# 2 MB expert-weight blocks in 11 slots, zero-padded attention keys, another order of the last w2 products and of the final norm

## Chip, cores and metric

One NeuronCore of one Trainium2 chip runs the whole block. The metric is the device time of one execution in microseconds (us), the median of several runs.

## What is computed

The reference is one encoder layer on 512 tokens of width 1024, in float32. What matters here:

```python
xn   = rms_norm(h, norm_mix_w)
proj = xn @ w_in                      # 1024 x 9728: q/k/v of 24 attention heads, retention q/k/v/gate, branch gates
# branch A: 3 groups of 8 heads (head size 64); group 0 a window of +-64 tokens in token order,
#           groups 1 and 2 over tokens of equal residue mod 4 (and 16, by a mask)
scores = q @ k.T / 8 ; p = exp(scores - max) ; out = p @ v      # denominators combine the three groups
# branch B: retention, then both branches are gated, merged and projected by w_out
h   = h + merged @ w_out
hn  = rms_norm(h, norm_moe_w)
# mixture of experts: 64 experts, two per token out of one group of 8
hid = silu(xb @ w1[e]) * (xb @ w3[e]) ; y = hid @ w2[e]         # w1, w3: 1024 x 512, w2: 512 x 1024 each
out = rms_norm(h + sum(gate * y), norm_final_w)
```

Every expert gets tokens, so the 64 x 3 weight matrices of 2 MB each (384 MB in blocks of 1024 x 1024 bytes) are read once.

## The kernel before, in words

**Mixer.** Every projection goes through `project` (lines 242 to 281): weights come in chunks of 256 x 512 (`raw`, 512 KB, two buffers, DMA issued by SyncE at line 103), ScalarE and VectorE split each into a rounded part and a remainder (lines 212, 213), and TensorE multiplies three times (lines 267 to 269 for token-major results, 273 to 275 for transposed ones). The normalised input lies transposed in four tiles `xH0`, `xH1`, `xL0`, `xL1`; the same four hold the retention result and then the merged branches.

**Attention.** Per head group g the program projects q and k transposed, applies rotary (`rotary_to`: line 314 on VectorE, 315 and 316 on GpSimd), projects v, and then works through the query tiles. One score product has a contraction of 64: for g = 1, 2 (line 639) one product of 128 columns per head, 64 in all, with the odd head of a pair in partitions 64 to 127; for g = 0 (line 595) products of 192 columns. `probs` (lines 551, 553) adds the mask, takes the maximum and the exponential, `transposed_probs` (line 557) transposes, line 648 multiplies by v. These steps are mixed by the framework's scheduler with the products of the next projection, so that TensorE's queue is a fixed list in which a score product stands between projection products.

**Experts.** `experts(g)` handles four experts (32 token places each) at a time, 16 times. The tokens are gathered by one-hot products (line 769) into `xT`; then come 16 blocks of w1 and w3 (line 973) and 8 blocks of w2 (line 1026), each block 1 MB: 128 partitions, each one run of 8 KB. `wtile` gives each block a slot: 11 of pool `wA`, 2 halves of `big` (used once, later the result tile), `xH0`, `xL0`, `xH1`, `xL1` and `wB`; 18 for the first pass, 16 afterwards. A slot is loaded again as soon as the products that read it are done. All loads are issued by SyncE in program order (line 936), and a load waits for the eighth load before it. The w2 blocks hold 128 output columns each (`columns`); after them the result is split in two parts (lines 1009, 1010) and spread back to the tokens (`scatter`, lines 1017 to 1019). The last four experts do this in five column pieces of 256, 256, 256, 128 and 128, each product followed at once by its spread, with `finish` (line 1061) squaring for the norm.

**End.** `final` sums the squares, takes the root on GpSimd (line 152), multiplies by the norm weight (lines 1097 to 1100) and stores in seven pieces (lines 1102 and 1112).

The pools of the first loads lie where the attention's tiles lay, so the first weight load (program order: after five loads of w_out) waits until the mixer's last readers are done.

Of the kernel before, what the change touches and what calls it, by code (L numbers as in the profile page):

```python
# [10 lines left out]
F32 = mybir.dt.float32  # L11
# [26 lines left out]
NWA = 11  # L38
NK2 = 4
# [29 lines left out]
def hybrid_block(ctx, tc, a, out):  # L69
# [86 lines left out]
    class Halves:  # L156


        def __init__(self):
            self.t = []  # L160
            for i in range(2):
                t_ = xp.tile([P, 4, S], F32R, name=self.tag + "01"[i])
                self.t.append(t_)
# [7 lines left out]
    class Hi(Halves):  # L171
        tag = "xH"

    class Lo(Halves):
        tag = "xL"
# [11 lines left out]
    xH = Hi()  # L187
    xL = Lo()
# [106 lines left out]
    def rotary_to(dst, dilated):  # L295
# [4 lines left out]
        def evac(b, ps):  # L300
# [8 lines left out]
            for k in range(2):  # L309
# [6 lines left out]
                nc.gpsimd.tensor_tensor(d, d, w, op=ALU.add)  # L316
# [228 lines left out]
    rec0 = at.tile([P, NT, REC], F32, name="rec0")  # L545
    orders = (nat, dil4, dil4)
# [15 lines left out]
    def windows(qT, kT, v4):  # L562
# [14 lines left out]
        for t in range(NT):  # L577
# [9 lines left out]
            for slot, hh in enumerate((0, 1, 4, 5)):  # L587
                po = (hh % 2) * HD
                ps = tmp()
                sm = rp.tile([P, 512], F32, name="sd", bufs=6)  # L590
                for i in range(2):
                    cs = slice(i * W, (i + 1) * W)
                    blk = hh // 2 + i
                    for qs, k0 in parts_:
                        nc.tensor.matmul(ps[qs, cs], qT[po:po + HD, blk, t * P + qs.start:t * P + qs.stop],
                                         kT[po:po + HD, blk, k0:k0 + W], start=True, stop=True)
                    probs(rec, hh + 2 * i, ps[:, cs], sm[:, cs], masks[:, mo_:mo_ + W])
                prT = transposed_probs(ps, sm, 3)
                oc = slice(slot * (HD + 1), (slot + 1) * (HD + 1))
                for i in range(2):  # L600
                    full = slice(2 * i * P, (2 * i + 1) * P)
                    po = i * HD
                    for qs, k0 in parts_:
                        nc.tensor.matmul(po_ps[i][qs, oc], prT[:, full][:, qs],
                                         values(k0 + po, 0, P, hh + 2 * i), start=True, stop=False)
                    for qs, k0 in parts_:
                        nc.tensor.matmul(po_ps[i][qs, oc], prT[po:po + HD, P:2 * P][:, qs],
                                         values(k0 + (1 - i) * P, po, HD, hh + 2 * i), start=False, stop=True)
            for i in range(2):
                nc.scalar.copy(rec[:, :NH * (HD + 1)].rearrange("p (x z w) -> p x z w", x=2, z=2)[:, :, i],  # L610
                               po_ps[i][:, :4 * (HD + 1)].rearrange("p (x w) -> p x w", x=2))

    for g in range(3):
        qT, kT = qk_tiles()
        project_in(512 * g, None, rotary_to(qT, g > 0))
        project_in(1536 + 512 * g, None, rotary_to(kT, g > 0))
# [8 lines left out]
        if g == 0:  # L625
            windows(qT, kT, v4)
# [538 lines left out]
```

## Time and profile before

| | |
|---|---|
| median of 3 runs | 1665.96 us (1661.69 to 1669.53) |
| the profiled execution | 1663.84 us, its span 1662.1 us |
| TensorE busy | 1386.6 us (83%), 11699 instructions |
| VectorE, ScalarE, GpSimd busy | 561.7, 328.7, 182.4 us |
| granted TensorE clock, mean | 0.913 |
| moved by DMA | 476.56 MB in 98509 packets |

The page cuts the span into 40 slices of 41.55 us. Read it first for which engine is full where, then look at the stretches one by one: a busy share over the whole span says little, because the mixer and the experts have different limits. In the timelines a float32 product shows as two instructions, a rounded one (fp32r) as one. SPq is SyncE's queue, its rows are the moments at which DMAs are issued.

### The profile page before, as it was taken

Reading aid. Unit: us, or ns where it says so; the run is one execution under the profiler, and the core shown is the slowest. Engines: PE = TensorE matmul, PEld = TensorE weight load, DVE = VectorE, ACT = ScalarE, POOL = GpSimd, SP = SyncE. Lnnn points to the kernel's source line nnn. Section 1 sums busy time; section 2 is a strip of 40 time slices with the busy share of each in tenths; the row PEclk is TensorE's granted clock in tenths of the full one; section 3 lists DMA queues with packets and bytes.
Section 4 is the critical chain, followed back from the end, with each engine's and each line's share of the span. In section 5 each row is a group of like instructions: output and inputs, shape, how many; then the busy total and the mean of one; then the engine's idle time right before and its main releaser. Section 6 shows DMA issues by size and latency. Waiting matters only on the chain. (4 is left out here: it accounts for less than half of the span.)

```text
span 1662.1 us, 27242 instructions
## 1 busy us (share of the span) xinstructions
PE 1386.6 (83%) x11699; PEld 915.9 (55%) x11699; DVE 561.7 (34%) x1241; ACT 328.7 (20%) x618; POOL 182.4 (11%) x137
## 2 busy tenths in 40 slices
PE   7999999999999999988776776776776786687674
PEld 6878787686876778754442442342353354244243
DVE  7556463554634544442220120120221121022014
ACT  5332334334346333210000000000000000000002
POOL 2214260231502211000000000000000000000001
PEclk9999999999999999998987887897898788888787
DMA  6324343233323423989999999999999999999995
GB/s 179 111 77 105 91 137 90 77 102 96 96 90 90 141 76 107 398 341 421 421 421 422 422 422 422 422 421 422 422 421 421 422 422 422 421 422 421 422 421 213
DMA packets 98509, 476.56 MB, mean 287 GB/s; under 512 B 17296, under 2 KB 17808, under 8 KB 49168
## 3 DMA queue, kind: packets, MB, share of 16 engines
q1 hardware_dynamic: 97344, 474.76, 72.8%
q8 instruction: 94, 1.54, 0.4%
q14 instruction: 31, 0.25, 0.0%
q10 hardware_dynamic: 1040, 0.00, 0.0%
HBM read 459.96 MB, written 4.26 MB: 279 GB/s over the span
## 5 line engine op out<-in xcount | busy, mean ns | idle before, releaser
L973 PE MATMUL acc<-wa,xT 128*32 128x512 f32 x1408 | 212.4, 716 | 83.7 <-DMA wa<-in_moe_w_dram 83.7
L213 DVE SCALAR_TENSOR_TENSOR wL<-raw,nwx,wH 128x512 fp32r<-128x512 f32 x152 | 138.0, 937 | 106.8 <-ACT wH L212 106.6
L268 PE MATMUL acc<-xL,wH 128*128 128x512 f32 x416 | 172.0, 413 | 0.0
L267 PE MATMUL acc<-xH,wH 128*128 128x512 f32 x416 | 168.8, 406 | 1.2 <-ACT kT L667 1.2
L973 PEld LDWEIGHTS acc<-wa,xT 128*32 128x32 f32 x1408 | 37.7, 117 | 237.2 <-DMA wa<-in_moe_w_dram 176.2
L269 PE MATMUL acc<-xH,wL 128*128 128x512 f32 x416 | 168.0, 404 | 0.0
L1026 PE MATMUL acc<-wa,k 128*32 128x128 f32 x2816 | 113.9, 319 | 56.8 <-DMA wa<-in_moe_w2c_dram 52.4
L1026 PEld LDWEIGHTS acc<-wa,k 128*32 128x32 f32 x2816 | 89.0, 129 | 81.2 <-DMA wa<-in_moe_w2c_dram 65.0
L212 ACT ACTIVATE wH<-raw,nwx 128x512 fp32r<-128x512 f32 x152 | 103.1, 716 | 150.1 <-PE acc L275 55.8
L273 PE MATMUL acc<-wH,xH 128*128 128x512 f32 x320 | 127.6, 400 | 0.2 <-ACT rt L536 0.2
L274 PE MATMUL acc<-wL,xH 128*128 128x512 f32 x320 | 127.5, 398 | 0.1
L275 PE MATMUL acc<-wH,xL 128*128 128x512 f32 x320 | 127.4, 398 | 0.0
L994 DVE SCALAR_TENSOR_TENSOR k<-k,gsl,acc 128x512 f32<-128x512 f32 x16 | 12.0, 748 | 332.8 <-issue 283.2
L769 PE MATMUL tmp<-oh,h 128*128 128x128 f32 x960 | 110.6, 276 | 0.3 <-DVE big L1019 0.3
L769 PEld LDWEIGHTS tmp<-oh,h 128*128 128x128 f32 x960 | 108.7, 192 | 3.7 <-DVE big L1019 3.2
L152 POOL TENSOR_TENSOR rr<-rv,mhalf 128x1 f32<-128x1 f32 x8 | 4.9, 622 | 947.0 <-ACT jk L1061 935.9
L1010 DVE TENSOR_TENSOR xT<-acc,xT 128x512 fp32r<-128x512 f32 (+2 forms) x35 | 22.6, 646 | 231.9 <-ACT xT L1009 231.8
L267 PEld LDWEIGHTS acc<-xH,wH 128*128 128x128 f32 x416 | 78.4, 189 | 22.4 <-issue 2.5
L268 PEld LDWEIGHTS acc<-xL,wH 128*128 128x128 f32 x416 | 78.5, 189 | 21.5 <-issue 2.3
L269 PEld LDWEIGHTS acc<-xH,wL 128*128 128x128 f32 x416 | 78.5, 189 | 18.1 <-issue 1.5
L1019 DVE TENSOR_TENSOR big<-big,tmp 128x512 f32<-128x512 f32 (+2 forms) x132 | 76.6, 635 | 21.7 <-PE tmp L1018 21.7
L1017 PE MATMUL tmp<-xT,k 128*128 128x512 f32 (+2 forms) x140 | 61.5, 462 | 22.9 <-ACT xT L1009 22.1
(259 smaller groups left out, 1705.3 us busy)
## 6 DMA issues: line engine op xcount, KB each, us to landing
wa<-in_moe_w_dram SPq DMA_DIRECT2D x176, 1024.0 KB, 19.8
wa<-in_moe_w2c_dram SPq DMA_DIRECT2D x88, 1024.0 KB, 19.9
raw<-in_w_in_dram SPq DMA_DIRECT2D x76, 512.0 KB, 3.7
xH<-in_moe_w_dram SPq DMA_DIRECT2D x32, 1024.0 KB, 19.8
xL<-in_moe_w_dram SPq DMA_DIRECT2D x31, 1024.0 KB, 19.7
xL<-in_moe_w2c_dram SPq DMA_DIRECT2D x16, 1024.0 KB, 19.8
xH<-in_moe_w2c_dram SPq DMA_DIRECT2D x16, 1024.0 KB, 19.8
wB<-in_moe_w_dram SPq DMA_DIRECT2D x15, 1024.0 KB, 19.6
```

Source lines behind the costliest of these rows:

```text
L212: nc.scalar.activation(wH[:, k, :], raw[:, k, :], AF.Copy, scale=sc)
L213: nc.vector.scalar_tensor_tensor(wL[:, k, :], raw[:, k, :], sc, wH[:, k, :], op0=ALU.mult, op1=ALU.subtract)
L267: nc.tensor.matmul(ps[tt], wh[:, cs], srcH.blk(kt), **fl)
L268: nc.tensor.matmul(ps[tt], wh[:, cs], srcL.blk(kt), start=False, stop=False)
L269: nc.tensor.matmul(ps[tt], wl[:, cs], srcH.blk(kt), start=False, stop=(kt == nk - 1))
L273: nc.tensor.matmul(ps[tt], aH, wh, **fl)
L274: nc.tensor.matmul(ps[tt], aH, wl, start=False, stop=False)
L275: nc.tensor.matmul(ps[tt], aL, wh, start=False, stop=(kt == nk - 1))
L769: nc.tensor.matmul(gp[j // 4][:, (j % 4) * P:(j % 4 + 1) * P], h[:, t, j * P:(j + 1) * P], oh_t.rearrange("p e c -> p (e c)"), start=(t == ...
L973: nc.tensor.matmul(p_[e * CAP:(e + 1) * CAP, :], xT[:, j, e * CAP:(e + 1) * CAP], wt[:, e * FF:(e + 1) * FF], start=(j == 0), stop=(j == N ...
L1019: nc.vector.tensor_tensor(hs_[:, t, cs], (h if first else hs_)[:, t, cs], ps, op=ALU.add)
L1026: nc.tensor.matmul(py[e * CAP:(e + 1) * CAP, o:o + P], hdT[:, i, e * CAP:(e + 1) * CAP], w4[:, e, i, :], start=(i == 0), stop=(i == 3))
```

## The change

1. **Blocks.** w1 and w3 of one 128-row stretch come in one block: 2 MB, each partition one run of 16 KB (8 per four experts). w2 comes in 4 blocks by rows of the contraction (`moe_w2r`), so that each product has 512 columns and the result is complete only after the fourth block; for the last four experts the w2 blocks still hold columns (`moe_w2c`, 256 each, the last one loaded in two halves).
2. **Slots.** 11 slots of 2 MB: 5 of `wA`, `big` and `wk` once, `x0`, `x1` (each now holds the rounded and the remainder half of four blocks), 2 of `wB`; 9 from the second pass on. `xT`, the split result, the transposed one-hots and the hidden values have one buffer each; the last four lie in the place of `wk` after the first experts.
3. **Padded keys.** Rotary writes the keys to `kP`, 128 partitions by block, parity and token, zero in the other head's half. One product with a contraction of 128 gives the scores of both heads (256 columns for g = 1, 2; 384 for g = 0). GpSimd writes the two halves separately and clears the zeros once.
4. **Last experts.** A column piece's product is issued ahead of the spread before it.
5. **End.** GpSimd multiplies by the norm weight in `finish`, for all but the last 128 columns; in the last piece the squares of two of the four token tiles go to VectorE; one root for all four tiles; four stores of 512 KB.

```diff
-NWA = 11
-NK2 = 4
+NWA = 5
+NWB = 2
+SLOT = 4096
...
-                nc.gpsimd.tensor_tensor(d, d, w, op=ALU.add)
+                if pad is None:
+                    nc.gpsimd.tensor_tensor(d, d, w, op=ALU.add)
+                else:
+                    for z in range(2):
+                        hp = slice(z * HD, (z + 1) * HD)
+                        nc.gpsimd.tensor_tensor(pad[hp, b - 1 + k, z, :], d[hp], w[hp], op=ALU.add)
...
+    kP = at.tile([P, 4, 2, S], F32, name="kP")
+    for z in range(2):
+        nc.gpsimd.memset(kP[(1 - z) * HD:(2 - z) * HD, :, z, :], 0.0)
...
+                ts = slice(t * P, (t + 1) * P)
+                for i in range(0, 4, 2):
+                    nc.tensor.matmul(ps[:, i * P:(i + 2) * P], qT[:, (h0 + i) // 2, ts], kP[:, (h0 + i) // 2, :, ts],
+                                     start=True, stop=True)
                 for i in range(4):
-                    hh = h0 + i
-                    po = (hh % 2) * HD
                     cs = slice(i * P, (i + 1) * P)
-                    ts = slice(t * P, (t + 1) * P)
-                    nc.tensor.matmul(ps[:, cs], qT[po:po + HD, hh // 2, ts], kT[po:po + HD, hh // 2, ts],
-                                     start=True, stop=True)
-                    probs(rec, hh, ps[:, cs], sm[:, cs], masks[:, 3 * HD:3 * HD + P] if g == 1 else masks[:, 9 * HD:])
+                    probs(rec, h0 + i, ps[:, cs], sm[:, cs],
+                          masks[:, 3 * HD:3 * HD + P] if g == 1 else masks[:, 9 * HD:])
...
-    spare = [(xp, "xH0"), (xp, "xL0"), (xp, "xH1"), (xp, "xL1"), (mo, "wB")]
+    ring = [(wA, "wa")] * NWA + [(xp, "x0"), (xp, "x1")] + [(mo, "wB")] * NWB
+    once = [(big, "big"), (wk, "wk")]
+    slots = ring[:NWA] + once + ring[NWA:]
...
         for j in range(NK):
+            wt = load(block(w13, g, j)).rearrange("p (w e f) -> p w e f", w=2, e=EG)
             for w_, p_ in enumerate((p1, p3)):
-                wt = load(block(w13, g, 2 * j + w_))
                 for e in range(EG):
...
         if cols is None:
+            py = [acc(), acc()]
+            for i in range(4):
+                wt = load(block(w2r, g, i)).rearrange("p (e d) -> p e d", e=EG)
+                for hf in range(2):
+                    for e in range(EG):
+                        nc.tensor.matmul(py[hf][e * CAP:(e + 1) * CAP, :], hdT[:, i, e * CAP:(e + 1) * CAP],
+                                         wt[:, e, hf * 512:(hf + 1) * 512], start=(i == 0), stop=(i == 3))
...
-            for c0, n in cols:
-                py = acc()
-                for o in range(0, n, P):
-                    columns(wts[(c0 + o) // P], py, o)
-                cs = slice(c0, c0 + n)
-                split(cs, py[:, :n], nc.vector if n < 256 else nc.scalar)
-                scatter([cs])
-                finish(c0, n)
+            waits = []
+            for c in cols:
+                if c == cols[-1]:
+                    while waits:
+                        spread(*waits.pop(0))
+                waits.append((*c, product(*c)))
+                if len(waits) > 1:
+                    spread(*waits.pop(0))
+            spread(*waits.pop(0))
...
+            if i < len(last) - 1:
+                nc.gpsimd.tensor_tensor(o[t][:, cs], x, wf[:, cs], op=ALU.mult)
...
+        def rows(tt, eng):
+            rt = r[:, tt:tt + 1]
+            ts = slice(tt * P, (tt + 1) * P)
+            nc.vector.scalar_tensor_tensor(o[tt][:, c0:], res[0][:, tt, c0:], rt, wf[:, c0:], op0=ALU.mult,
+                                           op1=ALU.mult)
+            if eng is nc.scalar:
+                nc.scalar.activation(o[tt][:, :c0], o[tt][:, :c0], AF.Copy, scale=rt)
             else:
...
+                eng.tensor_scalar(o[tt][:, :c0], o[tt][:, :c0], rt, None, op0=ALU.mult)
+            nc.sync.dma_start(out=out[0, ts, :], in_=o[tt])
```

How TensorE's list changes in head group 1, from one `v` product (line 648) to the transposes. `sd` are the probabilities, `acc` rows are projection products. Before:

```order
L648 MATMUL tmp<-v,sd 64x65 x8
L639 MATMUL tmp<-kT,qT 128x128
L268 MATMUL acc<-xL_111,wH 128x512
L269 MATMUL acc<-xH_109,wL 128x512
L267 MATMUL acc<-xH_109,wH 128x512
L639 MATMUL tmp<-kT,qT 128x128
L268 MATMUL acc<-xL_111,wH 128x512
L269 MATMUL acc<-xH_109,wL 128x512
L267 MATMUL acc<-xH_109,wH 128x512
L639 MATMUL tmp<-kT,qT 128x128
```

and with the change:

```order
L657 MATMUL tmp<-v,sd 64x65 x8
L645 MATMUL tmp<-kP,qT 128x256 x2
L268 MATMUL acc<-x_109,wH 128x512
L269 MATMUL acc<-x_109,wL 128x512
L267 MATMUL acc<-x_109,wH 128x512
L268 MATMUL acc<-x_109,wH 128x512
L269 MATMUL acc<-x_109,wL 128x512
L267 MATMUL acc<-x_109,wH 128x512
L567 MATMUL tmp<-ident,sd 128x128 x3
```

Four score products, three of them alone between projection products, have become two that follow the `v` products directly.

SyncE's queue from the mixer's last loads to the second use of a slot. `raw` are mixer weights, `wk`, `wa`, `big`, `x_`, `wB` slots. Before:

```order
L103 DMA raw<-in_w_out_dram 128x2x512 x5
L936 DMA wa<-in_moe_w_dram 128x2048 x2
L103 DMA raw<-in_w_out_dram 128x2x512
...
L936 DMA wa<-in_moe_w_dram 128x2048 x7
L936 DMA big<-in_moe_w_dram 128x2048 x2
L936 DMA xH_5711<-in_moe_w_dram 128x2048
L936 DMA xL_5717<-in_moe_w_dram 128x2048
L936 DMA xH_5723<-in_moe_w_dram 128x2048
L936 DMA xL_5773<-in_moe_w2c_dram 128x2048
L936 DMA wB<-in_moe_w2c_dram 128x2048
L936 DMA wa<-in_moe_w2c_dram 128x2048 x6
```

and with the change:

```order
L942 DMA wk<-in_moe_w_dram 128x4096
L105 DMA raw<-in_w_in_dram 128x2x512 x3
...
L105 DMA raw<-in_w_out_dram 128x2x512 x5
L942 DMA wa<-in_moe_w_dram 128x4096
...
L942 DMA wa<-in_moe_w_dram 128x4096 x3
L942 DMA big<-in_moe_w_dram 128x4096
L942 DMA x_5657<-in_moe_w_dram 128x4096
L942 DMA x_5713<-in_moe_w2r_dram 128x4096
L942 DMA wB<-in_moe_w2r_dram 128x4096 x2
L942 DMA wa<-in_moe_w2r_dram 128x4096
```

One block (`wk`) is now loaded ahead of the mixer's last 23 weight chunks; the other first-pass blocks keep their place, and each row moves twice the bytes.

## Rows read from the trace of the kernel before

**Rows 1.** The page's 40 slices: busy tenths of TensorE and of the DMA engines.

```profile
PE   7999999999999999988776776776776786687674
DMA  6324343233323423989999999999999999999995
```

**Rows 2.** Stretches around the start of the expert weights: from:to, length, busy us of PE, PEld, DVE, ACT, POOL with their instruction counts, granted TensorE clock, mean DMA share, GB/s.

```profile
661.50:705.70 44.20, 44.05 (x280) 34.34 (x279) 16.97 (x50) 14.11 (x26) 1.12 (x2) 1.00 0.96 390
705.70:710.50 4.80, 4.42 (x41) 3.52 (x40) 4.16 (x25) 1.29 (x4) 0.55 (x1) 1.00 0.21 51
...
718.00:721.50 3.50, 3.50 (x35) 1.75 (x37) 3.09 (x20) 1.38 (x10) 0.00 (x0) 1.00 0.22 54
721.50:1635.00 913.50, 673.30 (x7845) 359.34 (x7837) 157.72 (x340) 47.92 (x93) 0.00 (x0) 0.85 1.01 420
```

**Rows 3.** SyncE's queue around the same place: start, length of the issue (or of several), what is loaded.

```profile
661.50 0.82 SPq L936 DMA_DIRECT2D wa<-in_moe_w_dram  x2
674.40 4.82 SPq L936 DMA_DIRECT2D wa<-in_moe_w_dram  x7
...
692.99 0.33 SPq L936 DMA_DIRECT2D xH<-in_moe_w_dram  x1
...
709.20 0.33 SPq L936 DMA_DIRECT2D xH<-in_moe_w_dram  x1
...
720.19 4.62 SPq L936 DMA_DIRECT2D wa<-in_moe_w2c_dram  x6
```

**Rows 4.** DMA packets of three stretches, in this order: 800 to 1600 us (8 KB runs only, full), 664 to 674 us (8 KB runs and the 2 KB runs of w_out, full), and 640 to 660 us (2 KB runs alone, not full; its second line gives the share of the engines' time).

```profile
DMA packets 46309, 337.20 MB, mean 422 GB/s; under 512 B 5137, under 2 KB 5137, under 8 KB 5265
...
DMA packets 966, 4.11 MB, mean 411 GB/s; under 512 B 80, under 2 KB 80, under 8 KB 592
...
DMA packets 823, 1.60 MB, mean 80 GB/s; under 512 B 48, under 2 KB 48, under 8 KB 822
q1 hardware_dynamic: 822, 1.59, 23.8%
```

**Rows 5.** TensorE in head group 1: start, length (from the first start to the modelled end), line, tile shape, result.

```profile
378.55 0.69 PE L648 MATMUL tmp<-v,sd 128*64 128x65 f32 x16
379.16 0.49 PE L639 MATMUL tmp<-kT,qT 64*128 64x128 f32 x2
379.58 0.50 PE L268 MATMUL acc<-xL,wH 128*128 128x512 f32 x1
379.92 0.40 PE L269 MATMUL acc<-xH,wL 128*128 128x512 f32 x1
380.15 0.39 PE L267 MATMUL acc<-xH,wH 128*128 128x512 f32 x1
380.47 0.49 PE L639 MATMUL tmp<-kT,qT 64*128 64x128 f32 x2
380.89 0.50 PE L268 MATMUL acc<-xL,wH 128*128 128x512 f32 x1
```

**Rows 6.** Groups by line and shape: count, busy us, mean ns, idle time before.

```profile
L639 PE MATMUL tmp<-kT,qT 64*128 64x128 f32 x128 | 31.1, 323 | 0.2 <-DVE rec L551 0.2
L447 POOL MEMSET yret<- 64x1024 f32 x1 | 1.1, 1132 | 0.0
```

**Rows 7.** A run of full-array float32 products of 128 columns (the gather), and what starts after it.

```profile
1588.99 7.41 PE L769 MATMUL tmp<-oh,h 128*128 128x128 f32 x64
1596.33 4.50 PE L973 MATMUL acc<-wa,xT 128*32 128x512 f32 x40
```

**Rows 8.** Who TensorE waited for between 200 and 660 us, the longest in total: us, times, longest.

```profile
PE tmp L604 <- DVE sd L559: 1.7, 2, 1.3
```

**Rows 9.** GpSimd on the keys of head group 1.

```profile
343.88 4.86 POOL L315 TENSOR_TENSOR sw<-sw,ropeT 128x512 f32<-128x512 f32 x2 [11.24 <-DMA sw<-kT]
348.69 3.44 POOL L316 TENSOR_TENSOR kT<-kT,sw 128x512 f32<-128x512 f32 x2
...
356.87 3.44 POOL L316 TENSOR_TENSOR kT<-kT,sw 128x512 f32<-128x512 f32 x2
```

**Rows 10.** The end in order of time: the last weight load's issue, the additions of one spread of 256 columns, the last product, the last additions, the roots, the stores.

```profile
1623.38 0.33 SPq L936 DMA_DIRECT2D xH<-in_moe_w2c_dram  x1
...
1640.71 1.42 DVE L1019 TENSOR_TENSOR big<-big,tmp 128x256 f32<-128x256 f32 x4 [0.48 <-PE tmp L1018]
1644.04 1.08 PE L1026 MATMUL acc<-xH,k 128*32 128x128 f32 x32
1646.22 0.96 DVE L1019 TENSOR_TENSOR big<-big,tmp 128x128 f32<-128x128 f32 x4 [0.42 <-PE tmp L1018]
1647.66 2.16 POOL L152 TENSOR_TENSOR rr<-rv,mhalf 128x1 f32<-128x1 f32 x4 [935.87 <-ACT jk L1061]
1649.44 6.78 SPq L1102 DMA_DIRECT2D out_dram<-wa  x6
1656.31 0.38 SPq L1112 DMA_DIRECT2D out_dram<-wa  x1
```

**Rows 11.** DMA issues of the last expert blocks and of the stores: count, KB each, median us from issue to landing.

```profile
xH<-in_moe_w2c_dram SPq DMA_DIRECT2D x16, 1024.0 KB, 19.8
out_dram<-wa SPq DMA_DIRECT2D x2, 512.0 KB, 3.3
```

More of the change, by code (lines that the diff above doesn't have):

```diff
@@ L153, in rsqrt_begin, with __init__ @@
         return v, r
[L156 to L163, printed above, removed]
+    class Part:
+        def __init__(self, t):
+            self.t = t
         def blk(self, k):
@@ L169, in four, with hi_lo @@
             return self.t[b0 // 4]
[L171 to L175, printed above, removed]
+    def hi_lo():
+        t = []
+        for i in range(2):
+            t_ = xp.tile([P, 2, 4, S], F32R, name=f"x{i}")
+            t.append(t_)
+        return [Part([t_[:, z] for t_ in t]) for z in range(2)]
     class One:
@@ L922, in wtile @@
         nw[0] += 1
[L923 to L930 removed]
+        pool, tag = slots[i] if i < len(slots) else ring[(i - len(slots)) % len(ring)]
+        t_ = pool.tile([P, SLOT], F32, name=tag, bufs={"wa": NWA, "wB": NWB}.get(tag, 1))
         return t_
@@ L941, in block, with experts @@
         return w[bass.ds(g, 1), i:i + 1].rearrange("g i p n -> p (g i n)")
-    def experts(g, ranks, cols=None, first=False):
+    def experts(g, ranks, cols=None, first=False, ends=False):
         es = bass.ds(g * EG, EG)
@@ L1029, in experts, with product @@
         if cols is None:
-            css = [slice(0, 512), slice(512, D)]
-            for cs in css:
-                py = acc()
-                for b in range(4):
-                    columns(load(block(w2, g, cs.start // P + b)), py, b * P)
-                split(cs, py, nc.scalar)
+            py = [acc(), acc()]
[5 more added lines that the diff above has]
+                                         wt[:, e, hf * 512:(hf + 1) * 512], start=(i == 0), stop=(i == 3))
+            css = [slice(0, 512), slice(512, D)]
+            for cs, p_ in zip(css, py):
+                split(cs, p_, nc.scalar)
             scatter(css)
         else:
-            wts = [load(block(w2, g, b)) for b in range(NK)]
-            tail.enter_context(tc.manual_schedule(engines=all_engines))
-            for c0, n in cols:
+            wts = []
+            for b in range(NK // 2):
+                t_ = wtile()
+                src = w2c[b:b + 1].rearrange("b p n -> p (b n)")
+                for c in range(0, SLOT, SLOT // 2 if b == NK // 2 - 1 else SLOT):
+                    n = SLOT // 2 if b == NK // 2 - 1 else SLOT
+                    nc.sync.dma_start(out=t_[:, c:c + n], in_=src[:, c:c + n])
+                wts += [t_[:, :SLOT // 2], t_[:, SLOT // 2:]]
+            if ends:
+                tail.enter_context(tc.manual_schedule(engines=all_engines))
+                final_tiles()
+            def product(c0, n):
                 py = acc()
@@ L1044, in experts, with spread @@
                     columns(wts[(c0 + o) // P], py, o)
+                return py
+            def spread(c0, n, py):
                 cs = slice(c0, c0 + n)
@@ L1119, in hybrid_block @@
             nc.vector.tensor_scalar(ranks, ranks, float(CAP), None, op0=ALU.add)
-            with tc.For_i(0, NGRP, 1) as g:
+            with tc.For_i(0, NGRP - 1, 1) as g:
                 experts(g, ranks)
+            experts(NGRP - 1, ranks, cols=last)
+        final_tiles()
         for c0, n in last:
```

152 lines of the change are left out of this document (72 added, 80 removed).

## The prediction

> **What bounds the kernel now.** I read the 40 slices first [rows 1]: up to slice 16 TensorE stands at 9 and the DMA engines at 2 to 4, from slice 18 to slice 38 the DMA engines stand at 9 and TensorE at 7 to 8. So there are two kernels in one: a mixer that TensorE limits, and experts that the reading of 384 MB limits. The waits confirm the first: between 200 and 660 us the longest wait of TensorE, in total, is 1.7 us [rows 8]. The stretches confirm the second: from 721.5 us on, 420 GB/s at a DMA share of 1.01 without a break [rows 2], while TensorE is busy 673.3 of 913.5 us. Hence a microsecond taken from TensorE's list in the mixer brings the first expert load forward by one; in the experts only a faster or earlier stream counts, and then the tail behind the last byte.
>
> The seam: loads begin at 661.5 us [rows 3]. 15 blocks fill the engines to 705.7 (0.96), then the share falls to 0.21 until a slot of the merged tiles comes free at 709.2, three blocks follow, and again 0.22 until 720.2, when the first products have freed slots [rows 2, 3]. The end: the last load is issued at 1623.4 and lands 19.8 us later, at 1643.2 [rows 10, 11]; the last additions end at 1647.2 (3.9 us behind it), the span 14.9 us after that.
>
> **The change, part by part.**
>
> *Padded keys, head groups 1 and 2.* Of one round of four heads, one score product follows the v products and three stand alone [rows 5]. From L268 at 379.58 to L268 at 380.89 is 1.31 us for three projection products and one score product. The projection products start 0.23 us apart (379.92 to 380.15), so a lone score product costs 1.31 - 0.69 = 0.62 us; its two instructions of 128 columns need about 0.23 (7.34 us for 64 such instructions is 0.115 each [rows 7]), the rest is lost around it. The one behind the v products costs 0.42 plus 0.11 that the second product after it starts late: 0.53. A round: 0.53 + 3 x 0.62 = 2.39 us. Now two products of 256 columns, 4 instructions at 2 x 0.115 = 0.92 us, plus about 0.1 at one edge: 1.02. 128 instructions are 64 products or 16 rounds [rows 6]: 16 x 1.37 = 22 us less. For group 0 the columns stay the same and I count some five lone pieces fewer at 0.4 us lost each, -2 us. The other way: GpSimd writes the keys in two halves. If 64 partitions cost as much as 128 (1.72 us [rows 9]; at best half of it, and then nothing changes), a pair of key blocks takes 3.4 us more. In group 1 the second pair is then ready at 360.3 + 6.9 = 367.2 us; scores began at 364.2 there with the first pair, which would be ready at 355.6, and the second pair is wanted a round later, about 5 us. It just fits; I allow 3 us of waits over the three groups. Clearing the zeros is two fills of 2048 columns, 2 x 2.3 us from the fill of 1024 [rows 6], on a GpSimd that is 11% busy. Sum -21 us; bounds -3 (the softmax chain of four heads, now started at once, or the keys make TensorE wait) and -26.
>
> By the Trainium skill (TensorEngine Tiling (Array Packing), Performance Considerations) a contraction of at most 64 calls for two row tiles side by side, up to twice as fast; by that rule padding to 128 would give away 16 x 4 x 0.115 = 7 us instead of saving. The trace disagrees for this order: products of 64 rows stand alone here, and no second one runs beside them. The same page says (Key Properties) that a change of tiling mode drains the array, and that is what the 0.3 instead of 0.23 us before and after each lone product looks like.
>
> *Seam.* One block (`wk`, 2 MB) is read during the mixer, where the DMA share is 2 to 4 tenths; SyncE's three w_in chunks behind it come up to 5 us later, which the two raw and three split buffers cover (four chunks of 24 products at 0.23 us, 22 us). From 661.5 on: six blocks (12 MB) and three w_out chunks to about 695, `x0` (free at 693.0 as before) to 700.4, then nothing until `x1` at 709.2; with 1.5 us from issue to flow, the stream runs from 710.7 without a break, 16 MB being done, because 6 MB (`x1`, `wB`, `wB`) last to 725 and the first slot is free at 720.2. Before, 18 MB were done and the stream ran from 721.5; 16 MB done corresponds to 721.5 - 2 x 2.49 = 716.5. Gain 716.5 - 710.7 = -6 us; bounds -2 and -8.
>
> *Longer runs.* Data packets of 8 KB: (46309 - 5265) of them in 800 us x 16 engines, 0.312 us each, the small end-of-transfer packets included [rows 4]. In the mixed stretch 374 of these and 512 of 2 KB fill 160 engine-us: (160 - 116.7) / 512 = 0.085 us for 2 KB. A line through both has 0.009 us per packet and 0.0370 us per 1000 bytes: 0.615 us for 16 KB, against 0.624 for two of 8 KB, 1.4%. Of the 921.7 us from 721.5 to 1643.2 that is -13 us. Bounds: nothing, if the rate is a limit of bytes alone (the flat 422 GB/s of 800 us); and 4.2%, -39 us, with the 0.098 us of a lone 2 KB packet (23.8% of 320 engine-us over 774 packets [rows 4]), which is the farther row because those engines idle between packets. I take -13.
>
> *Ring and last experts.* The ring is 9 slots of 2 MB, 44 us of stream. At a group's end TensorE's list has the last w2 block, the spread, the gather (7.4 us [rows 7]) and only then the next block: about 2 + 1 + 6 + 7.4 + 1 = 17 us without freeing a slot, 3.5 blocks. Five remain in flight; no stall, cost nothing. If this cover went (over 39 us) it would show at each of 15 seams. w2 with 512 columns frees TensorE some us per group, which nobody waits for. At the very end the third product now needs a whole 2 MB block and the third spread stands behind the fourth product, so VectorE's additions (1.42 us per 256 columns, in order, [rows 10]) pile up behind the last two megabytes: last additions about 6 us after the last landing instead of 3.9, +2. Behind them: one root over four columns for 2.16 us in four, the weight already multiplied, last store issued some 5.7 us after the last additions instead of 9.1 (1656.3 - 1647.2). But four stores of 512 KB begin together and share the engines: last landing at about 10.8 against 9.1 + 3.3 = 12.4. -1. Net +1 us; bounds -4 and +4.
>
> Sum: -21 - 6 - 13 + 1 = -39 us on the profiled execution's 1663.8, which lies 2.1 us below the median: 1625 there, **1626 us** as a median.
>
> **Rivals.**
> 1. *The runs bring nothing* (also if a run of 16 KB is moved as two packets of 8 KB, so that the change does not do what it says). For it: 422 GB/s to three digits in every slice. Against: the mixed stretch carries 411 with half of its packets at 2 KB, so a packet has a price. Time 1626 + 13 = 1639. The Trainium skill (DMA: Bandwidth & Descriptors, Bandwidth) names 358 GB/s of HBM per core as what binds such reads, which would make run length idle; the trace reads 422 here, above it. Its other limit there, 435 GB/s for the ports, would allow 3%, an estimate by which the sum would come to 1611.
> 2. *The mixer does not shrink:* TensorE waits at the transposes for four exponentials in a row, or for GpSimd's keys. For it: the key pairs fit with nothing to spare. Against: six to nine projection products, 1.4 to 2.1 us, stand between scores and transposes. Only 3 us of 21 remain: 1644.
> 3. *Slower:* 16 KB strides between partitions make the 16 engines meet on the same part of the memory, and the stream falls. From -26 us of the other terms it decides at a loss of 2.8% (410 GB/s); at 5% the time is 1626 + 13 + 46 = 1685. For it: no row shows such runs. Against: from 2 to 8 KB the rate only rose. The same page (Latency and other measured facts) tells of rates that fall with row pitches of large powers of two; its loss at 512 KB is 3%, estimated by which 16 KB would lose less than that, and no run here shows it yet.
>
> **Numbers.** Forecast 0.62, rival 1 0.17, rival 2 0.12, rival 3 0.05, 0.04 for rivals 1 and 2 together (1657). A measurement of this kernel can tell about 0.5% (8 us) from no change. Faster needs under 1657.6: the forecast, rivals 1 and 2, half of the pair, less a little for what I have not seen: 0.91; within 0.5%: 0.04; slower: 0.05. The forecast's own range is 1612 to 1637; the range reaches up to rival 2 with 2 us, 1646, and down by half of the upper rate bound, 1604.
>
> **What would show it.** Right: first wide expert load at about 640 us instead of 661.5, one block much earlier; score products in pairs, no wait over 2 us on TensorE before it; 427 GB/s in the flat stretch and issues 4.92 us apart; a gap only before `x1`; last additions some 6 us behind the last landing. Wrong: TensorE waiting for keys or exponentials; 421 GB/s or less; DMA share under 1.0 between groups.

## The result, and the profile after

The changed kernel takes **1624.3 us** (median of 4 runs, 1622.0 to 1626.2) against 1664.7 for the kernel before on the same chip; ratio 0.9754, 95% interval 0.9727 to 0.9782. Forecast were 1626 and 1604 to 1646. The profiled execution took 1624.35 us, its span 1622.7. All medians here are of executions in the usual state; one execution of `undone_four` below, 1697 us at a mean granted clock of 0.82, is left out.

The 40 slices, busy tenths of TensorE and of the DMA engines, against [rows 1]:

```profile
PE   7999999999999999997886785776776676677575
DMA  6334253233434323899999999999999999999994
```

Counted from 0, the DMA engines stand at 9 without a break from slice 17 on; before, slice 17 was an 8 and the unbroken 9s began in slice 18. SyncE's queue around the seam, against [rows 3] (start, length of the issue, what is loaded):

```profile
525.33 0.33 SPq L942 DMA_DIRECT2D wk<-in_moe_w_dram  x1
641.54 0.34 SPq L942 DMA_DIRECT2D wa<-in_moe_w_dram  x1
...
673.25 0.33 SPq L942 DMA_DIRECT2D x<-in_moe_w_dram  x1
689.48 0.33 SPq L942 DMA_DIRECT2D x<-in_moe_w2r_dram  x1
689.91 0.84 SPq L942 DMA_DIRECT2D wB<-in_moe_w2r_dram  x2
```

The first wide load stands at 641.54 instead of 661.50, and one block (`wk`) 116 us ahead of it. The stretches, against [rows 2] (the last three columns are granted TensorE clock, DMA share, GB/s):

```profile
686.00:688.00 2.00, 1.86 (x23) 1.24 (x22) 1.54 (x12) 0.77 (x3) 0.55 (x1) 1.00 0.00 0
...
690.00:692.00 2.00, 2.00 (x23) 1.79 (x24) 1.50 (x11) 1.24 (x3) 0.55 (x1) 1.00 0.88 213
...
695.00:700.00 5.00, 4.64 (x47) 3.82 (x50) 4.10 (x19) 0.02 (x1) 0.00 (x0) 1.00 1.04 442
700.00:705.00 5.00, 5.00 (x52) 1.53 (x48) 4.67 (x38) 3.21 (x13) 0.00 (x0) 1.00 1.02 436
705.00:1580.00 875.00, 638.41 (x4777) 264.90 (x4769) 149.37 (x310) 42.77 (x76) 0.00 (x0) 0.87 1.01 428
```

One gap is left, ahead of `x1`; the second gap of before (718.0 to 721.5, share 0.22) is gone, and 420 GB/s have become 428 at the same share. The end in order of time, against [rows 10]: the second product, the first additions, the fourth and the fifth product, the last additions, the root, the stores.

```profile
1590.76 3.51 PE L1040 MATMUL acc<-wB,hid 128*32 128x128 f32 x64 [2.39 <-DMA wB<-in_moe_w2c_dram]
1594.75 1.41 DVE L1033 TENSOR_TENSOR big<-big,tmp 128x256 f32<-128x256 f32 x4 [5.43 <-PE tmp L1032]
1598.70 1.08 PE L1040 MATMUL acc<-wa,hid 128*32 128x128 f32 x32
1604.54 1.94 PE L1040 MATMUL acc<-wa,hid 128*32 128x128 f32 x32
1607.73 1.57 DVE L1033 TENSOR_TENSOR big<-big,tmp 128x128 f32<-128x128 f32 x4 [0.57 <-PE tmp L1032]
1610.40 1.02 POOL L154 TENSOR_TENSOR rr<-rv,mhalf 128x4 f32<-128x4 f32 x1 [3.88 <-DVE rv L152]
1613.78 2.86 SPq L1151 DMA_DIRECT2D out_dram<-wa  x4
```

The span cut at three points (the last weight packet's end is read from the DMA records, the others from the rows):

| us | before | changed | difference |
|---|---|---|---|
| start to first wide load | 661.5 | 641.5 | -20.0 |
| to the end of the last weight packet | 981.2 | 958.5 | -22.7 |
| to the end of the last additions | 4.5 | 9.2 | +4.7 |
| to the end of the span | 14.9 | 13.4 | -1.5 |
| span | 1662.1 | 1622.7 | -39.4 |

The prediction counts from the landing, the moment at which the last load is reported complete. Before, that is 1643.1 us, 0.4 us behind the end of the last weight packet. In the changed kernel's trace it is 1601.8, 1.8 us behind it: by the packet records a 16 KB instruction load of 1.10 us stands between one engine's last weight packet and the 4-byte packet that ends its part of the load. From the landing to the last additions it is therefore 4.1 us before and 7.5 us now.

### The profile page after: what moved, and what is told of

Its sections match the earlier page's. It is cut to its first block, busy times and chain, and to the rows that moved or that the text cites. A ratio compares the mean times of both kernels' runs of the same rounds, so it can differ in the third digit from the quotient of the medians.

```text
span 1622.7 us, 20926 instructions
## 1 busy us (share of the span) xinstructions
PE 1348.0 (83%) x8707; PEld 830.1 (51%) x8707; DVE 559.6 (34%) x1231; ACT 318.0 (20%) x611; POOL 213.4 (13%) x163
## 4 chain that ended last, share of the span: by engine, by line
PE 54%; DMA 38%; DVE 4%; ACT 1%; issue 1%; POOL 1%; SPq 0%; DVEq 0%; ACTq 0%; POOLq 0%
DMA wa<-in_moe_w2r_dram 22%; DMA x<-in_moe_w2r_dram 10%; PE acc L267 6%; PE acc L268 6%; PE acc L269 6%; PE tmp L778 6%; PE acc L979 5%; DMA wa<-in_moe_w_dram 4%; PE acc L275 4%; PE acc L273 4%; PE acc L274 4%; DMA wB<-in_moe_w2c_dram 2%; PE tmp L1031 2%; PE acc L1049 2%; PE tmp L1032 2%; PE tmp L645 1%
## 5 line engine op out<-in xcount | busy, mean ns | idle before, releaser
L979 PE MATMUL acc<-wa,xT 128*32 128x512 f32 x1120 | 158.7, 701 | 67.5 <-DMA wa<-in_moe_w_dram 67.5
L267 PE MATMUL acc<-x,wH 128*128 128x512 f32 x416 | 170.2, 409 | 3.5 <-ACT kT L676 3.5
L268 PE MATMUL acc<-x,wH 128*128 128x512 f32 x416 | 167.9, 404 | 0.0
L269 PE MATMUL acc<-x,wL 128*128 128x512 f32 x416 | 167.9, 403 | 0.0
L1049 PE MATMUL acc<-wa,hid 128*32 128x512 f32 x560 | 91.5, 785 | 52.5 <-DMA wa<-in_moe_w2r_dram 47.8
L275 PE MATMUL acc<-wH,x 128*128 128x512 f32 x320 | 127.8, 399 | 0.0
L273 PE MATMUL acc<-wH,x 128*128 128x512 f32 x320 | 127.6, 400 | 0.2 <-ACT rt L542 0.2
L274 PE MATMUL acc<-wL,x 128*128 128x512 f32 x320 | 127.4, 398 | 0.1
L267 PEld LDWEIGHTS acc<-x,wH 128*128 128x128 f32 x416 | 79.2, 190 | 23.7 <-ACT kT L676 3.9
L268 PEld LDWEIGHTS acc<-x,wH 128*128 128x128 f32 x416 | 78.8, 190 | 18.9 <-issue 1.4
L979 PE MATMUL acc<-wB,xT 128*32 128x512 f32 x480 | 64.6, 667 | 28.5 <-DMA wB<-in_moe_w_dram 28.4
L269 PEld LDWEIGHTS acc<-x,wL 128*128 128x128 f32 x416 | 78.9, 190 | 17.9 <-issue 0.2
L979 PE MATMUL acc<-x,xT 128*32 128x512 f32 x416 | 58.6, 699 | 29.4 <-DMA x<-in_moe_w_dram 29.4
```

The lines of the kernel that those rows point to most:

```text
L267: nc.tensor.matmul(ps[tt], wh[:, cs], srcH.blk(kt), **fl)
L268: nc.tensor.matmul(ps[tt], wh[:, cs], srcL.blk(kt), start=False, stop=False)
L269: nc.tensor.matmul(ps[tt], wl[:, cs], srcH.blk(kt), start=False, stop=(kt == nk - 1))
L273: nc.tensor.matmul(ps[tt], aH, wh, **fl)
L274: nc.tensor.matmul(ps[tt], aH, wl, start=False, stop=False)
L275: nc.tensor.matmul(ps[tt], aL, wh, start=False, stop=(kt == nk - 1))
```

## The experiments

The theory has three independent terms, each in a stage of its own (TensorE's list in the mixer, bytes done at the seam, price of a packet), less a longer tail. Its rivals are that the mixer's gain comes from waits, that the rate comes from fewer loads, and that the terms overlap. "Stream" below is the second row of the table above. Ratios are to the kernel before.

| run | median us | ratio (95%) | first wide load | stream |
|---|---|---|---|---|
| changed, again | 1625.35 | 0.9773 (0.9752 to 0.9794) | 640.9 | 959.8 |
| lone64 | 1643.08 | 0.9875 (0.9860 to 0.9890) | 661.3 | 958.2 |
| lone128 | 1626.48 | 0.9773 (0.9759 to 0.9786) | 643.4 | 958.3 |
| pair64 | 1617.91 | 0.9722 (0.9707 to 0.9736) | 634.6 | 958.2 |
| runs8k | 1636.07 | 0.9826 (0.9813 to 0.9840) | 643.5 | 971.5 |
| runs4k | 1658.15 | 0.9960 (0.9945 to 0.9976) | 645.7 | 991.5 |
| no_wk | 1629.75 | 0.9793 (0.9775 to 0.9811) | 642.5 | 963.3 |
| inorder | 1620.04 | 0.9738 (0.9725 to 0.9751) | 639.1 | 959.8 |
| p4_ahead | 1623.39 | 0.9754 (0.9740 to 0.9768) | 641.2 | 959.6 |
| undone_four | 1658.15 | 0.9960 (0.9947 to 0.9973) | 661.7 | 977.0 |
| pair64_inorder | 1613.83 | 0.9697 (0.9684 to 0.9711) | 634.4 | 958.3 |
| ret_pairs | 1612.74 | 0.9693 (0.9680 to 0.9705) | 633.6 | 958.2 |

### The keys: lone64, lone128, pair64

**lone64**

```diff
-                    nc.tensor.matmul(ps[:, i * P:(i + 2) * P], qT[:, (h0 + i) // 2, ts], kP[:, (h0 + i) // 2, :, ts], ...)
+                    nc.tensor.matmul(ps[:, cs], qT[po:po + HD, hh // 2, ts], kT[po:po + HD, hh // 2, ts], ...)
+                    # one per head, each followed by its probs; group 0 and rotary as before
```

> The changed kernel with the unpadded keys and the score products of before (64 rows, one per head, each between projection products), group 0 as before too; everything else as changed. My theory (a lone 64-row product between 128-row ones costs 0.53 to 0.62 us, the pair of padded ones 0.7 to 0.8 us for the round): first wide expert load at about 661 instead of 641.5, time +20 us, 1644 (ratio to before 0.988). Rival (the 20 us came from fewer waits, from the keys or the softmax): first wide load at 641 to 647, time +0 to +5 us.

Measured are 1643.1 us, 18.8 more than the changed kernel, with the first wide load at 661.3: with the old keys the mixer is as long as before, within 0.2 us. So the 20 us belong to the keys, and rival 2 of the prediction (the mixer does not shrink) falls.

**lone128**

```diff
+                    nc.tensor.matmul(ps[:, cs], qT[:, hh // 2, ts], kP[:, hh // 2, hh % 2, ts], ...)   # one per head
```

> The changed kernel with padded keys, but in head groups 1 and 2 one product of 128 columns per head, which the scheduler puts one by one between projection products as before; the same columns on TensorE in all. Theory A (the loss is the change between 64-row and 128-row products): a lone one costs 0.23 us, a round 0.92, first wide load at 641 to 645, time within +3 us of the changed kernel (1624 to 1627). Theory B (the loss is standing alone, whatever the rows): 0.53 to 0.62 each as before, first wide load at about 659, time +18 us, 1642.

Measured are 1626.5 us and a first wide load at 643.4, as theory A has it. TensorE in head group 1, first lone64, then lone128 (start, length to the modelled end, line, tile shape):

```profile
366.04 0.48 PE L646 MATMUL tmp<-kT,qT 64*128 64x128 f32 x2
366.45 0.50 PE L267 MATMUL acc<-x,wH 128*128 128x512 f32 x1
...
367.35 0.48 PE L646 MATMUL tmp<-kT,qT 64*128 64x128 f32 x2
```

```profile
364.48 0.41 PE L647 MATMUL tmp<-kP,qT 128*128 128x128 f32 x2
364.64 0.48 PE L267 MATMUL acc<-x,wH 128*128 128x512 f32 x1
...
365.42 0.40 PE L647 MATMUL tmp<-kP,qT 128*128 128x128 f32 x2
```

From one score product to the next, three projection products between, it is 1.31 us with 64 rows (that of [rows 5]) and 0.94 with 128. Less 0.70 for the three, the lone product costs 0.61 and 0.24. Both stand alone, both have the same columns. So the loss comes with the change between 64-row and 128-row products; a product of 128 rows that stands alone costs its two instructions (2 x 0.115 [rows 7]) and nothing more.

**pair64**

```diff
+                two = [ps, tmp()]
+                for i in range(4):      # even heads: rows 0 to 63, first bank; odd heads: rows 64 to 127, second bank
+                    nc.tensor.matmul(two[i % 2][:, i // 2 * P:(i // 2 + 1) * P], qT[po:po + HD, hh // 2, ts],
+                                     kT[po:po + HD, hh // 2, ts], start=True, stop=True)
```

> The changed kernel with unpadded keys; the four 64-row score products of a round stand directly behind one another, even heads into one PSUM bank, odd heads into another, so that neighbours use different halves of the rows; in group 0 two such products in place of one of 384 columns. Theory A (64-row products never run side by side here, and each change of row half or to 128 rows costs what a lone one shows): a round 0.92 us plus 0.3 at each edge, first wide load at 645 to 655, time +4 to +14 us. Theory B (two of different halves run side by side): 0.46 us of products plus the edges, a round about the 0.78 us of the changed kernel or less, first wide load at 637 to 641, time 0 to -5 us (1619 to 1624).

Measured are 1617.9 us, 6 us under the changed kernel, and a first wide load at 634.6. That is theory B, and more than it forecast. The same place in the changed kernel, then in pair64, from the `v` products to the second projection product:

```profile
367.82 0.69 PE L657 MATMUL tmp<-v,sd 128*64 128x65 f32 x16
368.44 1.13 PE L645 MATMUL tmp<-kP,qT 128*128 128x256 f32 x4
369.22 0.58 PE L268 MATMUL acc<-x,wH 128*128 128x512 f32 x1
369.64 0.40 PE L269 MATMUL acc<-x,wL 128*128 128x512 f32 x1
```

```profile
367.24 0.69 PE L659 MATMUL tmp<-v,sd 128*64 128x65 f32 x16
367.86 0.72 PE L647 MATMUL tmp<-kT,qT 64*128 64x128 f32 x8
368.50 0.50 PE L268 MATMUL acc<-x,wH 128*128 128x512 f32 x1
368.84 0.39 PE L269 MATMUL acc<-x,wL 128*128 128x512 f32 x1
```

1.82 us against 1.60. Eight instructions one after the other would need 8 x 0.115 = 0.92 us [rows 7]; from their start to L268 it is 0.64 with both edges: neighbours in different halves run side by side. In the prediction I held the Trainium skill's rule (TensorEngine Tiling (Array Packing), Overview, Theoretical Speedup: up to twice as fast for a dimension of at most 64) to be idle here. It was so only for the order of before; put side by side, in two banks, the trace agrees with it (0.64 us for eight instructions, against 0.92 one after the other).

The pairs themselves are the smaller part of the 6.9 us at the first wide load. Fourteen of the 16 rounds follow `v` products and gain 0.22 each, 3 us; by the starts of the same projection products pair64 is 2.0 us ahead at 514 us, when all rounds are done, in spite of 0.9 us that it lost to a lower clock near 145 us. At 525 it is 7.1 us ahead. The 5 us between are a wait of 3.5 us that the changed kernel has and pair64 has not, and a lower clock after it (waits of TensorE, of ScalarE, and SyncE's queue, of the changed kernel):

```profile
PE acc L267 <- ACT kT L676: 3.5, 1, 3.5
```

```profile
ACT wH L212 <- DMA raw<-in_w_in_dram: 12.6, 2, 7.0
```

```profile
503.34 8.67 SPq L697 DMA_DIRECT2D rec<-scr  x4
```

Around 512 us SyncE's queue is held by loads of `rec`, a weight chunk goes out behind them, ScalarE waits 7.0 us for it, and the gate's sigmoid, for which TensorE waits, stands behind that on ScalarE. It is not GpSimd's keys. Why the order falls out so was not tried. Behind the wait TensorE runs at a granted clock of 0.50 for some microseconds. Two traces with the same mixer, the changed kernel and inorder (below), whose wait was 2.7 us and whose clock stayed up:

```profile
520.00:525.00 5.00, 5.00 (x18) 4.00 (x18) 3.49 (x5) 1.34 (x2) 3.00 (x2) 0.78 0.36 112
```

```profile
520.00:525.00 5.00, 5.00 (x23) 4.02 (x22) 3.49 (x5) 0.86 (x2) 2.77 (x2) 1.00 0.36 105
```

Eighteen projection products against 23 in the same 5 us: with the end of the 515 to 520 stretch the clock costs the changed kernel some 1.4 us.

**ret_pairs** (on top of pair64_inorder, below) is the same idea in the retention:

```diff
+                for n in range(NT):
+                    for z in range(2):      # heads hh and hh + 1: two row halves, two banks
+                        nc.tensor.matmul(two[z][:, cs], kT[hp, hh // 2, cs], qT[hp, hh // 2, cs], start=True, stop=True)
```

> The version with both edits (score products of 64 rows in neighbouring pairs, product and spread in turn, 1613.8), and the 32 products of 64 rows of the retention, until now four in a row in the same half of the rows, put in pairs of different halves and two PSUM banks. Theory (neighbours of different halves run side by side): 64 instructions of 0.115 us become as long as 32, first wide load 3.7 us earlier, at about 631, time 1610. Rival (the second bank makes TensorE wait for VectorE, which reads them one after the other): first wide load at 634 or later, time 1614 to 1620.

First pair64_inorder, then ret_pairs:

```profile
122.77 1.16 PE L506 MATMUL tmp<-kT 64*128 64x128 f32 x8
```

```profile
122.25 1.16 PE L508 MATMUL tmp<-kT 64*128 64x128 f32 x16
```

Sixteen instructions take the 1.16 us of eight, which shows the mechanism by itself. But the first wide load moves by 0.8 us only and the medians' intervals overlap. Of ret_pairs' waits, the first has doubled (1.1 in pair64_inorder) and the second is new; and the clock of 145 to 150 us, which is 1.00 in pair64_inorder, is at its lower level (0.50):

```profile
PE tmp L517 <- DVE mv L525: 2.2, 1, 2.2
...
PE tmp L508 <- POOL kT L318: 0.7, 1, 0.7
```

```profile
145.00:150.00 5.00, 4.37 (x27) 4.08 (x25) 1.29 (x2) 0.00 (x0) 4.23 (x3) 0.50 0.41 119
```

The mechanism of the theory holds, its 3.7 us do not: the waits (1.8 us more) and the lower clock behind them take most of it back.

### The runs: runs8k, runs4k

```diff
-        nc.sync.dma_start(out=t_, in_=src)
+        nc.sync.dma_start(out=t_.rearrange("p (c n) -> p c n", c=2), in_=src)     # c=4 in runs4k
+        # the block lies in DRAM as c x 128 runs
```

> The changed kernel, each 2 MB load as before the chip one load, but its block laid out in DRAM as two halves of 128 runs of 8 KB; slots, order and number of loads as changed. Theory (a packet has a price of its own, 16 KB in 0.613 us against 2 x 0.312): flat stretch 422 GB/s, time +13 to +15 us, 1638 (ratio to before 0.984). Rival (fewer loads and fewer end packets, not the run length, made 428 GB/s): 426 to 428 GB/s, time 0 to +3 us.

> The same with four quarters of 128 runs of 4 KB. Theory by the line through 2 KB and 8 KB of the trace of before (0.009 us per packet, 0.0370 us per 1000 bytes): 0.161 us a packet, 0.642 us for 16 KB, 408 GB/s, time +43 us, 1667 (ratio 1.00). Rival (the loss from 16 to 8 KB is a step, e.g. rows that change place in memory, and no price per packet): as with 8 KB, 422 GB/s, 1638.

Packets of 800 to 1550 us: the changed kernel, runs8k, runs4k.

```profile
DMA packets 22147, 321.01 MB, mean 428 GB/s; under 512 B 2456, under 2 KB 2456, under 8 KB 2584
```

```profile
DMA packets 41139, 316.89 MB, mean 423 GB/s; under 512 B 2424, under 2 KB 2424, under 8 KB 2552
```

```profile
DMA packets 77905, 309.79 MB, mean 413 GB/s; under 512 B 2371, under 2 KB 2371, under 8 KB 77870
```

runs8k has as few loads and end packets (2424) as the changed kernel and yet falls to 423, about the 422 of before [rows 4], whose end packets are twice as many: the run length makes the rate, and the last 1 GB/s is all that is left for the number of loads. The stream is 13.0 us longer, the median 11.8; the theory had 13 to 15. runs4k gives 413, not the 408 of the line, and 33 us where 43 were expected; the direction is the theory's, the size is not. 16 KB on each of 16 engines take 262,144 bytes / 428 GB/s = 0.6125 us, 0.620 and 0.635 at the other two rates: 0.007 us for each packet more, where my line had 0.009. The rival of a single step falls.

### The seam: no_wk

```diff
-    once = [(big, "big"), (wk, "wk")]
-    slots = ring[:NWA] + once + ring[NWA:]
+    slots = ring[:NWA] + [(big, "big")] + ring[NWA:]
```

> The changed kernel without the early block: 10 slots in the first pass, the eighth w1/w3 block goes to x1. Theory (2 MB less are done when the stream restarts at x1, everything else stays): from the first wide load to the last landing 4.9 us more than the 958 us of the changed kernel, time +5 us, 1629. Rival (the seam does not matter, the last group waits for TensorE's list anyway): within 1 us of 958.

Measured are a stream of 963.3, 4.8 us more, and 1629.75 us, 5.5 more, as the theory has it. At the seam a block that is read earlier is worth its whole time on the engines (2 MB at 428 GB/s are 4.9 us).

### The tail: inorder, p4_ahead, and the changed kernel again

```diff
             for c in cols:
-                if c == cols[-1]:           # p4_ahead: only these three lines go
-                    while waits:
-                        spread(*waits.pop(0))
-                waits.append((*c, product(*c)))
-                if len(waits) > 1:
-                    spread(*waits.pop(0))
-            spread(*waits.pop(0))
+                spread(*c, product(*c))     # inorder
```

> The changed kernel with each w2 product of the last four experts followed at once by its spread, the order of before. Theory (the fifth product stands behind the fourth spread and TensorE idles 1600 to 1604 with the last block landed at about 1600, so the new order costs): last additions end about 6 us behind the last landing instead of 9.5, time -3 to -4 us (1620 to 1621). Rival (the new order saves, as the products then wait for VectorE's splits of the spread before): 0 to +4 us.

> The changed kernel, where the fifth of the last products too is issued ahead of the fourth spread. If it is only the fifth product's place behind the fourth spread that costs: as with product and spread in turn, 1620 to 1621. If every product ahead of a spread delays VectorE's additions: 1622 to 1624, last additions 7 to 9 us behind the last landing.

> The changed kernel again, unedited, in five rounds, as the base for the small differences (four runs so far, 1622.0 to 1626.2). If the order of the last products costs about 4 us, it lies at 1623 to 1626, above the 1618.6 to 1622.6 of the version with product and spread in turn; if that difference came from the spread of four runs, at 1620 to 1622. In the profile the distance from the last landing to the last additions follows the granted clock of the last 10 us: 9 us with a stretch at the low level as before, 6 to 7 without.

inorder is faster: 1620.0 against 1624.3 and 1625.4 of the changed kernel, and 1613.8 against 1617.9 when pair64 is there too. So the new order costs 4 to 5 us. In the traces not all of that lies in the tail: inorder's first wide load stands at 639.1, 2.5 us before the changed kernel's, by the shorter wait and the higher clock around 520 us that pair64's section shows, which this edit does not touch. pair64 and pair64_inorder have no such wait there, and the order is worth as much between them. inorder's second product and its last additions:

```profile
1588.14 1.95 PE L1040 MATMUL acc<-wB,hid 128*32 128x128 f32 x64
...
1601.86 0.96 DVE L1033 TENSOR_TENSOR big<-big,tmp 128x128 f32<-128x128 f32 x4 [0.42 <-PE tmp L1032]
```

In the changed kernel the first spread has its operands by 1589.3, but stands behind the second product, which waits 2.39 us for `wB`; then that product takes 3.51 instead of 1.95 us, at a granted clock of 0.50, the lower of the two levels (1.2 GHz), after a stretch in which TensorE had mostly waited:

```profile
1588.00:1590.00 2.00, 0.37 (x16) 0.10 (x4) 0.42 (x1) 0.37 (x1) 0.00 (x0) 1.00 1.00 422
...
1592.00:1594.00 2.00, 2.00 (x48) 1.80 (x40) 0.00 (x0) 0.00 (x0) 0.00 (x0) 0.50 0.64 266
```

The first additions begin at 1594.75 and everything follows from there; the fifth product stands behind the fourth spread and starts at 1604.54, 2.7 us after its weights have landed. In inorder the first spread fills the wait, and its second product takes 1.95. p4_ahead lifts only the fifth product. Its median, 1623.4, is the 1622 to 1624 of the second case, only 1 to 2 us under the changed kernel and inside the intervals; in its profiled execution (1621.05, the shortest of its four) the additions end 5.3 us behind the last weight packet, which was not expected there. So that place alone is not shown to explain the 4 us; how much of the rest is the first spread's place and how much the granted clock, these runs do not separate: in the profiled execution of pair64_inorder the clock was low before the tail began, and its last additions came 8.3 us behind the last weight packet in spite of the order, against 3.9 in inorder and 5.2 in ret_pairs with the same order.

The changed kernel again took 1625.4 us, inside the 1623 to 1626 expected if the order costs. What was expected of its trace does not hold as it stands. The second product meets the low clock here too, and yet the last additions end 6.1 us behind the last weight packet (5.7 behind the landing) and not 9. The fifth product is what differs:

```profile
1589.95 3.18 PE L1040 MATMUL acc<-wB,hid 128*32 128x128 f32 x64 [2.07 <-DMA wB<-in_moe_w2c_dram]
...
1603.58 1.08 PE L1040 MATMUL acc<-wa,hid 128*32 128x128 f32 x32
```

From the start of the fifth product to the end of the last additions it is 3.1 us here and 4.8 in the first trace, where the clock had fallen a second time (0.56 in 1604 to 1606, 1.00 here) and this product took 1.94 us.

### Together: undone_four, and the two faster edits

undone_four is lone64, no_wk and inorder in one, with each 2 MB block loaded as two loads of 1 MB in 8 KB runs. Beside the diffs above:

```diff
-        nc.sync.dma_start(out=t_, in_=src)
+        for c in range(2):
+            nc.sync.dma_start(out=t_[:, c * (SLOT // 2):(c + 1) * (SLOT // 2)], in_=src[c])
```

> Four parts of the change taken back together: unpadded keys with lone score products, 8 KB runs in loads of 1 MB (two per slot), no early block, each last product followed at once by its spread. Left of the change: 10 and then 9 slots of 2 MB, w2 products of 512 columns, the new end. If the parts act in separate stages their single effects add up: 1624.3 + 18.8 (unpadded keys) + 11.8 (8 KB runs) + 2 (twice the end packets, an estimate) + 5.5 (no early block) - 4.2 (order of the tail) = 1658, ratio to before 0.996. If they overlap or the slots cost something: 1650 or less, or 1664 and more.

Measured are 1658.2 us against 1658 by the sum: the terms add up, they do not overlap. What is left of the change is worth 6 us. At the seam (first two rows undone_four, in the order of the windows above):

```profile
704.00:706.00 2.00, 1.95 (x10) 1.29 (x10) 1.83 (x9) 0.28 (x1) 0.00 (x0) 1.00 0.02 8
...
715.00:720.00 5.00, 4.65 (x45) 3.98 (x47) 4.10 (x17) 0.00 (x0) 0.00 (x0) 1.00 1.03 429
```

```profile
704.00:706.00 2.00, 1.94 (x11) 1.33 (x11) 1.88 (x9) 0.51 (x1) 0.00 (x0) 1.00 0.76 320
...
715.00:720.00 5.00, 4.64 (x47) 3.81 (x49) 4.12 (x18) 0.04 (x1) 0.00 (x0) 1.00 0.66 274
```

The lower pair is the kernel before: it reads until about 706 and then runs dry a second time after 715; with 20 MB of slots the first gap comes earlier and the second not at all. By the packet records the first 30 MB are in 86.3 us after the first wide load, against 87.3 before: 1 us in sum. Another 2.4 us lie in the flat stretch (422.3 against 421.4 GB/s from 740 to 1590 us), about 0.8 at the very end of the stream (last section) and 1.8 in the new end. Part of the flat stretch's gain is the shorter program: 43 instruction loads of about 1.05 us during the stream where the kernel before has 65, which makes an estimated 22 x 1.05 / 16 = 1.4 us on 16 engines.

**pair64_inorder** joins the two faster edits.

> Both edits that were faster than the changed kernel: score products of 64 rows in neighbouring pairs, and each of the last w2 products followed at once by its spread. If they act in separate stages they add up: -6 and -4 us, 1614 (ratio to before 0.970). If the first moves the stream so that the tail falls otherwise: 1616 to 1620.

Measured are 1613.8 us: the two add up. With ret_pairs' 1612.7 these are the fastest versions, 0.97 of before; the two can't be told apart.

## Why the prediction was right, step by step

- *Padded keys, -21:* -20.0 at the first wide load. By the starts of the same projection products the changed kernel is 0.9 us ahead of the kernel before when the first scores of group 1 come, and 23.0 us ahead when the last of group 2 are done: the rounds bring the 22 us of the sum. Group 0 brings next to nothing of its 2, and why is open. The 3 us that I allowed for waits came (19.3 us ahead are left at 525), but from a late weight chunk and the low clock behind it, not from the keys; that this number fits is luck. GpSimd's 64-partition additions take 1.64 us, nearly as long as 128 partitions [rows 9], as the worst case had it, and nobody waited for them. "No wait over 2 us" failed by that one wait.
- *Seam, -6:* 30 MB are in 81.5 us after the first wide load, against 87.3: -5.8. The early block is 4.8 of it (no_wk), the second gap 1.0. The stream runs on from 690.5, 49 us after the first wide load, as worked out.
- *Longer runs, -13:* 428 GB/s. From 30 to 390 MB the changed kernel needs 14.2 us less than the kernel before; runs8k, the reverse, needs 11.2 more in that stretch and 13.0 in the whole stream. The remaining 3 us are mostly those of the flat stretch of undone_four, which the sum did not have. Rival 1 (runs bring nothing) falls with it, and rival 3 (16 KB strides slow the stream) falls at 428. The Trainium skill's 358 GB/s of HBM per core (DMA: Bandwidth & Descriptors, Bandwidth) binds nothing here: the trace has 428.
- *Ring, 0:* the windows hold 1.01 from 705 to 1580: no stall.
- *Tail, +1:* the additions end 7.5 us behind the last landing in the profiled execution and 5.7 in the second trace, where 6 were forecast and 4.1 measured before; the end behind them is 1.5 and 1.0 us shorter. The term is +1.9 and +0.6, so its size was right, but its mechanism was not. I had let VectorE's additions queue behind the last two megabytes. In the rows every group of additions waits for TensorE, whose queue holds a product that waits for its weights ahead of a spread that is ready; what that place costs and what the clock costs is not separated.
- The sum, counted to the landing: -20.0 at the first wide load, -21.3 from there to the landing (seam, longer runs and the shorter program, less the late end of the last load), +3.4 and -1.5 behind it, together -39.4. The forecast's -39 on the median of before, 1666.0, would be 1627 and not 1626; that slip of 1 us changes nothing.

## What to carry to other kernels

Look at the tile shapes in TensorE's list: 64-row products alone between 128-row ones cost far more than their columns. First try to put two of different row halves next to each other, in two PSUM banks; padding to 128 rows comes close to it (0.22 us a round, 3 us here) and takes most of the loss away. Look at the granted clock behind a wait of a few microseconds: the wait's price can be more than its length. When a fixed queue is reordered so that an item goes ahead of another, ask what the item in front waits for: a product issued early that waits for a DMA holds back work that is ready.

## What the runs showed of the hardware

- A change from 128-row to 64-row products and back costs about 0.37 us of TensorE per lone product (0.61 against 0.24).
- After waits of 2.2 us (ret_pairs), 2.4 us (the changed kernel again) and 3.5 us (the changed kernel) in the mixer TensorE's granted clock stood at 0.50 for 3 to 7 us; after one of 2.7 us (inorder) it stayed at 1.00. No run here tells why.
- In the last microseconds of the stream only half of the DMA engines have work, in every kernel here. First the changed kernel, then the kernel before:

```profile
1594.00:1596.00 2.00, 1.79 (x32) 1.38 (x27) 1.25 (x4) 0.80 (x4) 0.70 (x2) 1.00 0.48 201
```

```profile
1639.00:1641.00 2.00, 1.43 (x20) 0.96 (x12) 0.72 (x2) 0.37 (x1) 0.00 (x0) 1.00 0.49 201
```

By the DMA records a share near 0.5 lasts 8.5 us in the changed kernel and 13 in the kernel before, which is 4.1 and 6.1 us more than if all engines ended together; in the runs of this study with 2 MB slots it is 8 to 9.5. Which engines these are, and why they are behind after 900 full microseconds, no run here tells.
